# Windowed attention in a hybrid encoder layer: 192 keys for the query blocks at the grid's edges, and a moved weight copy

## The chip, the core and the metric

The kernel runs on one core of one Trainium2 chip. A core has TensorE (matmuls and transposes, results in PSUM), VectorE, ScalarE, GpSimd and SyncE, each with its own queue of instructions that it takes in order, and 16 DMA engines. The metric is device time in microseconds for one call; lower is better. In the profile TensorE is PE (its weight loads PEld), VectorE DVE, ScalarE ACT, GpSimd POOL, SyncE SP.

## The reference

One encoder layer over 512 tokens of width 2048, seen as a grid of 8 rows and 64 columns. A normalised input goes through one projection whose columns feed two groups: a gated convolution of width 31, and attention with 16 heads of 64 channels. Both are normalised, concatenated, projected and added to the residual; a gated MLP with a convolution of width 3 follows. The part that the change touches is the attention. As the grid has 8 rows and the window is 8 high, every query sees all rows, and 16 columns of them:

```python
col_start = np.clip(cols - kw // 2, 0, GRID_W - kw)        # kw = 16, GRID_W = 64
col_idx = col_start[:, None] + np.arange(kw)[None, :]
...
scores = jnp.einsum("bchd,bicjhd->bchij", q_row, k_win).astype(jnp.float32)
scores = scores + jnp.transpose(bias, (2, 0, 1, 3))[None]
p = jax.nn.softmax(scores.reshape(b, GRID_W, h, kh * kw), axis=-1)
...
return jnp.einsum("bchij,bicjhd->bchd", p, v_win)
```

A query in columns 0 to 15 sees columns 0 to 22 at most, one in columns 48 to 63 columns 40 to 63.

## The kernel before

Everything is computed in fp32 accuracy. A weight matrix is split into a rounded high part and the rest, its low part (`parts`, L129: the high part `whi` by ScalarE, L133, the low part `wlo` by VectorE, L134), the activations likewise (xh, xl), and three matmuls are added (`group`, L146: high by high L150, high by low L151, then eight low by high L153). A weight tile of 1024 columns, called a unit here, takes 24 matmuls. `weights` (L172) makes units AHEAD = 3 ahead of their use; `whi` and `wlo` have NW = 4 buffers each, the raw weights and the bias tables share NR = 9, and tiles of 2 KB a partition share NT = 75 (`t2`).

The order of the work: the projection runs unit by unit, in the order of ORDER (a letter a for a channel tile of the convolution, q for a pair of heads). After each unit, `tick` (L158) advances one step of the waiting generators, so attention work is put between units: `attend(p, ...)` for head pair p (0 to 7) and, after pair 5's projections, `group_a` (the convolution's normalisations). The convolution's 31 taps are handed to VectorE four at a time, behind each `wlo`. The tile framework then schedules each engine's instructions by priority; `pin` keeps some of them in program order, `tc.issue_after` puts the instructions of a block behind a given one, and `shifted` changes priority.

Attention for one pair of heads. The 64 columns are cut into 4 blocks of 16 columns; a query block is 16 columns by 8 rows, 128 queries. Keys and values lie in 8 groups of 8 columns (64 keys each), two groups to a chunk of 128. Each query block takes four groups, 256 keys: KEYS names for a block where they begin, in `k` itself for blocks 0 and 3, in `ks`, a copy with exchanged groups, for blocks 1 and 2. The steps:

- `turned_v` (L471): four transposes turn v; ScalarE copies it whole to vt[0] (L480) and with exchanged halves to vt[1] (L482, two copies).
- `scores` (L484): two query blocks by two heads at a time, 128 queries by 256 keys each, blocks 0 and 1 in one tile of two PSUM banks, blocks 2 and 3 in two further banks (L488).
- `softmax` (L494), for each bank (one head, two blocks, 512 wide): scaling and bias from a table on VectorE (L499), maximum (L501), two exponentials with sums on ScalarE (L504), reciprocal (L505), two scalings on ScalarE (L507).
- three ticks later (four for pairs 5 and 6), `turn` (L512): 16 transposes of 128 by 128 (L517), and `turned_p` (L521): four ScalarE copies `pt` of 512 (L525).
- one tick later, `values` (L528): 16 matmuls (L534) into one bank `po`, two chunks for each block and head, then ScalarE's copy (L572) and the split for the output projection.

The bias tables: two loads a pair on SyncE's queue (L543), each two heads by two blocks by 256 keys. Their content is laid out on the host.

Around the change: `group_a` sums the channels (L407) and adds over partitions by a matmul (L410), then squares (L222) and their sum (L261, a matmul in the bank tagged sc or tr), a root (L237), and a broadcast by matmul (L252) with a ScalarE copy (L254; the one named ra uses the bank tagged po, that of the values). L366 and L370 are the first projection at the start of the kernel. The output projection follows in `out_half`, whose matmuls have the same lines 150 to 153 and write `po`; the residual's tiles are loaded at L596. The MLP takes the time from about 600 us on (L746, L885).

Of the kernel before, what the change touches and what calls it, by code (L numbers as in the profile page):

```python
# [1 line left out]

# [1 line left out]

# [18 lines left out]
DH = 64  # L23
NA = 1024
CK = 31
WH = 8
WW = 16
# [25 lines left out]
NEG = -1.0e30  # L53
# [23 lines left out]
def layer(ctx: ExitStack, tc: tile.TileContext, xT, xn, w_0, w_in, w_out, w_up, w_down, par, tab, g3, out):  # L77
    nc = tc.nc
# [18 lines left out]

    def t4(shape, name):

        return wpool.tile(shape, F32, tag="raw", name=name, bufs=NR)  # L100
# [10 lines left out]
    def pc(name, i):  # L111
        o = POFF[name] + i
        return prm[:, o:o + 1]
# [6 lines left out]
    ps = psm.tile([P, S], F32, tag="mm", name="warm")  # L120
    for _ in range(WARM):
        nc.tensor.matmul(ps[:, :P], ones, ones, start=True, stop=True)
    ident = consts.tile([P, P], F32, name="ident")
    make_identity(nc, ident)

    def raw_unit(src, n):
        raw = t4([P, U * P], "raw")
        return raw, nc.sync.dma_start(raw[:, :n], src)

    def parts(raw, n):  # L130
        hi = wpool.tile([P, U * P], F32R, tag="whi", name="whi", bufs=NW)
        lo = wpool.tile([P, U * P], F32R, tag="wlo", name="wlo", bufs=NW)
        i = nc.scalar.activation(hi[:, :n], raw[:, :n], AF.Copy)  # L133
        j = nc.vector.tensor_sub(lo[:, :n], raw[:, :n], hi[:, :n].bitcast(F32))  # L134
# [9 lines left out]
    tight, taps = [], []  # L144

    def group(ps, ws, ms, first, last):  # L146

# [62 lines left out]
    def split(src, g, name):  # L210

        h, l = t2(name + "h", F32R), t2(name + "l", F32R)
        nc.scalar.activation(h, src, AF.Copy, scale=g)
        nc.vector.scalar_tensor_tensor(l, src, g, h.bitcast(F32), op0=ALU.mult, op1=ALU.subtract)
        return h, l

    def sum_sq(acc, src, first, to=slice(0, S)):
        if first:
            nc.scalar.activation(acc, src, AF.Square)
        else:  # L220
            q = t2("sq")[:, to]
            nc.scalar.activation(q, src, AF.Square)  # L222
            nc.vector.tensor_add(acc, acc, q)
# [42 lines left out]
    pin = tc.keep_in_program_order  # L266
# [170 lines left out]
    def grid(t, c0, w):  # L437
        return t.rearrange("p (r c) -> p r c", c=GW)[:, :, c0:c0 + w]

    def qkv(p):  # L440
# [23 lines left out]
            got.append(t)  # L464
        return got

    def attend(p, q, ks, v):


        hps = [slice(j * DH, (j + 1) * DH) for j in range(2)]  # L470
        vt, soft = [], []  # L471

        def turned_v():
            ps = psa.tile([P, NB, P], F32, tag="po", name="trv")
            for c in range(NB):
                m = nc.tensor.transpose(ps[:, c, :], v[:, c * P:(c + 1) * P], ident)
# [3 lines left out]
            nc.scalar.activation(vt[0], ps, AF.Copy)  # L480
            for hp, by in zip(hps, (slice(1, NB), slice(0, NB - 1))):
                nc.scalar.activation(vt[1][hp, :NB - 1], ps[hp, by], AF.Copy)  # L482

        def scores(b0, both, more=False):  # L484
            for i in range(2):
                b = b0 + i
                for j, hp in enumerate(hps):
                    m = nc.tensor.matmul(both[j][:, i, :], q[hp, b * P:(b + 1) * P],  # L488
                                         ks[KEYS[b][0]][hp, KEYS[b][1] * P:][:, :2 * P],
                                         start=True, stop=True)  # L490
                    if more or i or j:
                        pin(m)

        def softmax(both):  # L494
            two = tabs.pop(0)
            for j in range(2):
                tb = two[:, j]
                s = t2("s").rearrange("p (i k) -> p i k", i=2)
                nc.vector.scalar_tensor_tensor(s, both[j], DH ** -0.5, tb, op0=ALU.mult, op1=ALU.add)  # L499
# [8 lines left out]
                soft.append(s)  # L508

        pts = []  # L510

        def turn(two, more=False):  # L512
            for j in range(2):
                s, ps = soft.pop(0), two[j]
                for i in range(2):
                    for ch in range(2):
                        m = nc.tensor.transpose(ps[:, 2 * i + ch, :], s[:, i, ch * P:(ch + 1) * P], ident)  # L517
                        if more or i or j or ch:
                            pin(m)

        def turned_p(two):  # L521
            for ps in two:
                pt = t2("pt").rearrange("p (c k) -> p c k", c=4)
                with shifted(-SOONER):
                    nc.scalar.activation(pt, ps, AF.Copy)  # L525
                pts.append(pt)

        def values(po, b0, more=False):  # L528
            for i in range(2):
                b = b0 + i  # L530
                for ch in range(2):
                    for j in (1, 0):
                        hp = hps[j]
                        m = nc.tensor.matmul(grid(po, b * BLK, BLK)[hp], vt[KEYS[b][0]][:, KEYS[b][1] + ch, hp],  # L534
                                             pts[b0 + j][:, 2 * i + ch, :], start=(ch == 0), stop=(ch == 1))
                        if more or (i, ch, j) != (0, 0, 1):
                            pin(m)

        tabs = []

        def table(b0):
            tb = t4([P, 2, 2, 2 * P], "tab")
            i = nc.sync.dma_start(tb, tab[2 * p:2 * p + 2, :, b0 // 2:b0 // 2 + 2].rearrange("h p k c -> p h k c"))  # L543
            if p == 0:
                pin(i)
            tabs.append(tb)

        table(0)
        table(2)
        yield  # L550
        both = psa.tile([P, 2, 2, 2 * P], F32, tag="sc", name="sc")
        both = [both[:, j] for j in range(2)]
        more = [psa.tile([P, 2, 2 * P], F32, tag="tr", name="sc", bufs=2) for _ in range(2)]
# [8 lines left out]
        both = [both[:, j] for j in range(2)]  # L562
# [12 lines left out]
        yield  # L575

    p, n = -1, 0
# [407 lines left out]
    b = four(False)  # L985
# [6 lines left out]
    b = four(False)  # L992
# [83 lines left out]
```

## Time and profile before

| | |
|---|---|
| three timed runs | 1977.12, 1975.62, 1975.71 us; median 1975.71 |
| the profiled execution | 1976.0 us; span 1974.2 us |
| TensorE busy in the span | 1960.6 us |
| VectorE, ScalarE busy | 1611.7, 1105.8 us |
| matmuls of the scores (L488), busy | 10.4 us on k and 8.2 us on ks |
| transposes of the probabilities (L517), busy | 15.3 us |
| matmuls of the values (L534), busy | 15.7 us |

How to read it: busy is the time in which an engine worked on at least one instruction. Matmuls overlap in a pipeline, so the distance of their starts tells more than their lengths. A row of a timeline has the start in us from the span's start, the length, engine, line, operation, tiles written and read, sizes and count; in brackets stands the idle time before it and what ended that. In a group's row the count stands behind the x, then busy us and mean ns of one, then idle us before them and what ended those. The attention's pieces lie between 117 and 546 us.

### The profile page before, as it was taken

How to read it: one execution, taken by the hardware profiler on the slowest of the kernel's cores; microseconds unless marked ns; L12 is line 12 of the kernel's file. 1: busy time of each engine (PE TensorE's matmuls, PEld its weight loads, DVE VectorE, ACT ScalarE, POOL GpSimd, SP SyncE). 2: the span in 40 equal slices, each digit the busy share in tenths (PEclk: the TensorE clock that was granted, in tenths of full speed). 3: DMA queues.
4: the chain of work that ended last, by engine and by line, in shares of the span. 5: the costliest groups of instructions: out<-in, count | busy, mean ns of one | idle time of the engine just before them, and what ended most of it. 6: DMA issues, size and time to landing. Idle time of an engine off the chain costs nothing.

```text
span 1974.2 us, 27655 instructions
## 1 busy us (share of the span) xinstructions
PE 1960.6 (99%) x10141; PEld 1668.0 (84%) x10141; DVE 1611.7 (82%) x2338; ACT 1105.8 (56%) x1750; POOL 225.7 (11%) x310
## 2 busy tenths in 40 slices
PE   9999999999999999999999999999999999999998
PEld 7888888888788888888888888888888888888886
DVE  5987688787547888888989898988888898886765
ACT  6244424548525666666666666666666654554654
POOL 0111111111001111111111111111110400000000
PEclk9999999999999999999999999999999999999999
DMA  9776767766758889999999999999986977665663
GB/s 369 186 204 177 189 184 193 181 192 215 254 139 216 207 237 267 248 260 259 249 261 249 265 246 272 245 268 242 268 225 177 377 243 233 222 213 192 192 202 118
DMA packets 141817, 450.98 MB, mean 228 GB/s; under 512 B 15088, under 2 KB 23536, under 8 KB 140272
## 3 DMA queue, kind: packets, MB, share of 16 engines
q1 hardware_dynamic: 88880, 293.46, 43.8%
q0 software_dynamic: 42624, 148.92, 35.0%
q10 hardware_dynamic: 10176, 6.83, 1.1%
q8 instruction: 80, 1.31, 0.3%
q14 instruction: 57, 0.47, 0.1%
HBM read 430.27 MB, written 111.15 MB: 274 GB/s over the span
## 4 chain that ended last, share of the span: by engine, by line
PE 98%; DVE 1%; ACT 0%; DMA 0%; issue 0%; ACTq 0%; DVEq 0%
PE pu L746 43%; PE pd L885 21%; PE pj L150 7%; PE pj L151 7%; PE pj L153 7%; PE po L150 3%; PE po L151 3%; PE po L153 3%; PE po L534 1%; PE sc L488 1%; PE trp L517 1%; PE pj L366 1%; DMA we<-in_w 0%; PE trx L641 0%; PE pj L370 0%; DVE acc L407 0%
## 5 line engine op out<-in xcount | busy, mean ns | idle before, releaser
L133 ACT ACTIVATE whi<-raw 128x1024 fp32r<-128x1024 f32 x573 | 604.8, 1057 | 563.7 <-PE pj L151 166.6
L134 DVE TENSOR_TENSOR wlo<-raw,whi 128x1024 fp32r<-128x1024 f32 x573 | 699.5, 1222 | 232.5 <-ACT whi L133 192.0
L746 PE MATMUL pu<-xc,whi 128*128 128x512 f32 x2464 | 593.6, 391 | 0.0
L746 PEld LDWEIGHTS pu<-xc,whi 128*128 128x128 f32 x2464 | 451.3, 188 | 86.8 <-DVE xc L634 0.4
L746 PEld LDWEIGHTS pu<-xc,wlo 128*128 128x128 f32 x2464 | 319.2, 191 | 13.7
L746 PE MATMUL pu<-xc,wlo 128*128 128x256 f32 x2464 | 324.2, 283 | 0.0
L885 PE MATMUL pd<-whi,ho 128*128 128x512 f32 x1232 | 305.0, 389 | 0.1
L885 PEld LDWEIGHTS pd<-whi,ho 128*128 128x128 f32 x1232 | 231.1, 188 | 48.7 <-DVE vl L759 0.5
L150 PE MATMUL pj<-xh,whi 128*128 128x512 f32 x608 | 239.0, 393 | 0.0
L151 PE MATMUL pj<-xl,whi 128*128 128x512 f32 x608 | 236.9, 390 | 0.0
L392 DVE SCALAR_TENSOR_TENSOR y<-ch,prm,y 128x500 f32<-128x500 f32 (+14 forms) x240 | 177.3, 742 | 5.3
L885 PE MATMUL pd<-wlo,ho 128*128 128x512 f32 x616 | 165.1, 389 | 0.0
L153 PE MATMUL pj<-xh,wlo 128*128 128x512 f32 x608 | 150.3, 389 | 0.0
L150 PEld LDWEIGHTS pj<-xh,whi 128*128 128x128 f32 x608 | 114.1, 188 | 26.7 <-issue 2.8
L885 PEld LDWEIGHTS pd<-wlo,ho 128*128 128x128 f32 x616 | 115.6, 188 | 24.1
L153 PEld LDWEIGHTS pj<-xh,wlo 128*128 128x128 f32 x608 | 114.1, 188 | 23.7
L151 PEld LDWEIGHTS pj<-xl,whi 128*128 128x128 f32 x608 | 114.2, 188 | 23.6 <-issue 0.2
L755 ACT ACTIVATE pu<-pu 128x512 f32<-128x512 f32 x132 | 76.5, 580 | 92.9 <-PE pu L746 92.9
L695 POOL DMA_DIRECT2D raw<-in_w_up x88 | 78.0, 887 | 357.8 <-DVE wlo L134 206.7
L205 POOL DMA_DIRECT2D ws<-in_w_down x88 | 79.8, 907 | 309.1 <-DMA ws<-in_w_down 123.2
L202 POOL DMA_DIRECT2D ws<-ws x44 | 23.0, 524 | 318.1 <-PE pj L153 105.9
L202 POOL DMA_DIRECT2D ws<-in_w_down x44 | 22.9, 520 | 312.8 <-PE pj L153 172.9
(189 smaller groups left out, 1980.6 us busy)
## 6 DMA issues: line engine op xcount, KB each, us to landing
raw<-in_w_up SPq DMA_DIRECT2D x220, 512.0 KB, 5.9
ws<-in_w_down POOLq DMA_DIRECT2D x132, 512.0 KB, 6.1
raw<-in_w_up POOLq DMA_DIRECT2D x88, 512.0 KB, 7.4
raw<-ws SPq DMA_DIRECT2D x88, 512.0 KB, 4.2
raw<-in_w_in SPq DMA_DIRECT2D x76, 512.0 KB, 5.2
raw<-in_w_down SPq DMA_DIRECT2D x66, 512.0 KB, 3.8
ws<-ws POOLq DMA_DIRECT2D x44, 512.0 KB, 5.8
raw<-in_w_out SPq DMA_DIRECT2D x32, 512.0 KB, 5.3
```

The lines of the kernel that those rows point to most:

```text
L133: i = nc.scalar.activation(hi[:, :n], raw[:, :n], AF.Copy)
L134: j = nc.vector.tensor_sub(lo[:, :n], raw[:, :n], hi[:, :n].bitcast(F32))
L150: nc.tensor.matmul(ps, hi, mh, start=first and k == 0, stop=False)
L151: nc.tensor.matmul(ps, hi, ml, start=False, stop=False)
L153: i = nc.tensor.matmul(ps, lo[:, wk * P:(wk + 1) * P], mh, start=False, stop=last and k == len(ws) - 1)
L202: behind(nc.gpsimd.dma_start(wsum[c][k], a), ins)
L205: nc.gpsimd.dma_start(wsum[c][k], w_down[k, {1: A21, 2: A11, 4: A11, 6: A12}[c]], accum_op=ALU.add, max_dma_last_dim=ROW)
L392: nc.vector.scalar_tensor_tensor(y[:, a:b], h[:, a + j - PAD:b + j - PAD], prm[:, o:o + 1], y[:, a:b], op0=ALU.mult, op1=ALU.add)
L695: nc.gpsimd.dma_start(a[c], w_up[f, q2], accum_op=ALU.add)
L746: i = nc.tensor.matmul(ps[:, :n], part[:, k * P:(k + 1) * P], comb[c][k][:, :n], start=j == 0 and not more, stop=j == 2 * U - 1, skip_grou ...
L755: nc.scalar.activation(to, ps, AF.Copy)
L885: m = nc.tensor.matmul(ps[i], h[:, o + t * P:o + (t + 1) * P], w[:, d], start=start and not more and kind == 0 and j == 0, stop=stop and k ...
```

## The change

Five edits, all shown in the diff (cut):

1. The query blocks at the grid's edges, 0 and 3, take three groups of keys (192) instead of four; the middle blocks, 1 and 2, keep 256. The pairs of blocks that share a bank are now the two edge blocks (2 x 192 = 384 wide) and the two middle blocks (512).
2. The edge pair's probabilities are turned in three chunks of 128 for each head instead of four, 14 transposes a pair of heads instead of 16. The middle one of the three holds keys of both edge blocks. For it v is kept in a tile `edge` whose second and third chunks are zero in one half of the partitions; this tile is cleared once, and takes the place of vt[0]. ScalarE writes it in three copies (128x256, and twice 64x128) instead of one of 128x512. The values still take 16 matmuls.
3. The bias table holds the edge blocks (384) and one middle block (256) for each head; both middle blocks read the same one. It is loaded in two DMAs as before.
4. `turned_p` remembers its last copy in `copies`; the next weight unit's high part is issued after it on ScalarE.
5. The host lays out the table accordingly.

In the instructions as built, TensorE has 9907 instead of 9923, ScalarE 1708 instead of 1692. Ahead of the first of a pair's pt copies ScalarE has one high part fewer than before, in pair 6 three fewer; from the output projection's second half on, the order on every engine is the old one.

```diff
-KEYS = ((0, 0), (1, 0), (1, 1), (0, 2))
-WITHIN = ((0, 1, 2, 3), (1, 0, 3, 2))
+EDGE, MID = (0, 3), (1, 2)
+KEYS = ((0, 0, 3 * DH), (1, 0, 4 * DH), (1, 2 * DH, 4 * DH), (0, 5 * DH, 3 * DH))
+ATEDGE = ((0, 0), (1, 1)), ((1, 2), (2, 3))
+ATMID = ((0, 0), (1, 1)), ((2, 1), (3, 2))
...
-        i = nc.scalar.activation(hi[:, :n], raw[:, :n], AF.Copy)
+        with tc.issue_after(copies.pop().ins) if copies else nullcontext():
+            i = nc.scalar.activation(hi[:, :n], raw[:, :n], AF.Copy)
...
+    edge = t2("edge").rearrange("p (c k) -> p c k", c=NB)
+    nc.vector.memset(edge, 0.0)
...
-            vt.extend(t2("vt").rearrange("p (c k) -> p c k", c=NB) for _ in range(2))
-            nc.scalar.activation(vt[0], ps, AF.Copy)
-            for hp, by in zip(hps, (slice(1, NB), slice(0, NB - 1))):
+            vt.extend((edge, t2("vt").rearrange("p (c k) -> p c k", c=NB)))
+            nc.scalar.activation(edge[:, ::NB - 1], ps[:, ::NB - 1], AF.Copy)
+            for n, (hp, by) in enumerate(zip(hps, (slice(1, NB), slice(0, NB - 1)))):
+                nc.scalar.activation(edge[hp, n + 1], ps[hp, n + 1], AF.Copy)
                 nc.scalar.activation(vt[1][hp, :NB - 1], ps[hp, by], AF.Copy)
...
-                    m = nc.tensor.matmul(both[j][:, i, :], q[hp, b * P:(b + 1) * P],
-                                         ks[KEYS[b][0]][hp, KEYS[b][1] * P:][:, :2 * P],
+                    m = nc.tensor.matmul(both[j][:, i, :], q[hp, b * P:(b + 1) * P], ks[swapped][hp, at:at + w],
...
-                for i in range(2):
-                    for ch in range(2):
-                        m = nc.tensor.transpose(ps[:, 2 * i + ch, :], s[:, i, ch * P:(ch + 1) * P], ident)
+                for c in range(ps.shape[1]):
+                    m = nc.tensor.transpose(ps[:, c, :], s[:, c * P:(c + 1) * P], ident)
...
                 with shifted(-SOONER):
-                    nc.scalar.activation(pt, ps, AF.Copy)
+                    i = nc.scalar.activation(pt, ps, AF.Copy)
                 pts.append(pt)
+            copies[:] = [i]
...
-                        m = nc.tensor.matmul(grid(po, b * BLK, BLK)[hp], vt[KEYS[b][0]][:, KEYS[b][1] + ch, hp],
-                                             pts[b0 + j][:, 2 * i + ch, :], start=(ch == 0), stop=(ch == 1))
+                        m = nc.tensor.matmul(grid(po, b * BLK, BLK)[hp], vt[KEYS[b][0]][:, g, hp],
+                                             pt[j][:, c, :], start=n == 0, stop=n == 1)
...
-        table(0)
-        table(2)
+        we, wm = KEYS[0][2], KEYS[1][2]
+        te, tm = t4([P, 2, 2 * we], "tab"), t4([P, 2, wm], "tab")
+        for tb, at in ((te, slice(0, 2 * we)), (tm, slice(2 * we, None))):
+            i = nc.sync.dma_start(tb, tab[2 * p:2 * p + 2, :, at].rearrange("h p k -> p h k"))
...
-        scores(0, both, True)
-        scores(2, more, True)
-        softmax(both)
-        softmax(more)
+        scores(EDGE, both, True)
+        scores(MID, more, True)
+        softmax(both, we, lambda j: te[:, j].rearrange("p (i k) -> p i k", i=2))
+        softmax(more, wm, lambda j: tm[:, j].unsqueeze(1).broadcast_to([P, 2, wm]))
...
-        both = [both[:, j] for j in range(2)]
+        both = [both[:, j, :3] for j in range(2)]
...
-        values(po, 0)
-        values(po, 2, True)
+        values(po, EDGE, pts[:2], ATEDGE)
+        values(po, MID, pts[2:], ATMID, True)
```

More of the change, by code (lines that the diff above doesn't have):

```diff
@@ L1 @@
-from contextlib import ExitStack, contextmanager
+from contextlib import ExitStack, contextmanager, nullcontext
 import numpy as np
@@ L142, in unit @@
         return parts(raw_unit(src, n)[0], n)[:2]
-    tight, taps = [], []
+    tight, taps, copies = [], [], []
     def group(ps, ws, ms, first, last):
@@ L478, in turned_v, with scores @@
                     pin(m)
[L479 to L481 removed]
+            vt.extend((edge, t2("vt").rearrange("p (c k) -> p c k", c=NB)))
+            nc.scalar.activation(edge[:, ::NB - 1], ps[:, ::NB - 1], AF.Copy)
+            for n, (hp, by) in enumerate(zip(hps, (slice(1, NB), slice(0, NB - 1)))):
+                nc.scalar.activation(edge[hp, n + 1], ps[hp, n + 1], AF.Copy)
                 nc.scalar.activation(vt[1][hp, :NB - 1], ps[hp, by], AF.Copy)
[L484 to L486 removed]
+        def scores(pair, both, more=False):
+            for i, b in enumerate(pair):
+                swapped, at, w = KEYS[b]
                 for j, hp in enumerate(hps):
[L488 to L489 removed]
+                    m = nc.tensor.matmul(both[j][:, i, :], q[hp, b * P:(b + 1) * P], ks[swapped][hp, at:at + w],
                                          start=True, stop=True)
@@ L492, in scores, with softmax @@
                         pin(m)
-        def softmax(both):
-            two = tabs.pop(0)
+        def softmax(both, w, tb):
             for j in range(2):
-                tb = two[:, j]
-                s = t2("s").rearrange("p (i k) -> p i k", i=2)
-                nc.vector.scalar_tensor_tensor(s, both[j], DH ** -0.5, tb, op0=ALU.mult, op1=ALU.add)
+                flat = t2("s")[:, :2 * w]
+                s = flat.rearrange("p (i k) -> p i k", i=2)
+                nc.vector.scalar_tensor_tensor(s, both[j], DH ** -0.5, tb(j), op0=ALU.mult, op1=ALU.add)
                 nm = sm.tile([P, 2], F32, tag="nm", name="nm")
@@ L514, in turn @@
                 s, ps = soft.pop(0), two[j]
-                for i in range(2):
-                    for ch in range(2):
-                        m = nc.tensor.transpose(ps[:, 2 * i + ch, :], s[:, i, ch * P:(ch + 1) * P], ident)
-                        if more or i or j or ch:
-                            pin(m)
+                for c in range(ps.shape[1]):
+                    m = nc.tensor.transpose(ps[:, c, :], s[:, c * P:(c + 1) * P], ident)
+                    if more or c or j:
+                        pin(m)
@@ L521, in turned_p @@
         def turned_p(two):
             for ps in two:
-                pt = t2("pt").rearrange("p (c k) -> p c k", c=4)
+                pt = t2("pt")[:, :ps.shape[1] * P].rearrange("p (c k) -> p c k", k=P)
                 with shifted(-SOONER):
-                    nc.scalar.activation(pt, ps, AF.Copy)
+                    i = nc.scalar.activation(pt, ps, AF.Copy)
                 pts.append(pt)
[L528 to L531, printed above, removed]
+            copies[:] = [i]
@@ L532, in values @@
+        def values(po, pair, pt, places, more=False):
+            for i, b in enumerate(pair):
+                for n, (c, g) in enumerate(places[i]):
                     for j in (1, 0):
                         hp = hps[j]
-                        m = nc.tensor.matmul(grid(po, b * BLK, BLK)[hp], vt[KEYS[b][0]][:, KEYS[b][1] + ch, hp],
-                                             pts[b0 + j][:, 2 * i + ch, :], start=(ch == 0), stop=(ch == 1))
-                        if more or (i, ch, j) != (0, 0, 1):
+                        m = nc.tensor.matmul(grid(po, b * BLK, BLK)[hp], vt[KEYS[b][0]][:, g, hp],
+                                             pt[j][:, c, :], start=n == 0, stop=n == 1)
+                        if more or (i, n, j) != (0, 0, 1):
@@ L544, in table @@
             if p == 0:
                 pin(i)
-            tabs.append(tb)
-        table(0)
-        table(2)
         yield
-        both = psa.tile([P, 2, 2, 2 * P], F32, tag="sc", name="sc")
-        both = [both[:, j] for j in range(2)]
-        more = [psa.tile([P, 2, 2 * P], F32, tag="tr", name="sc", bufs=2) for _ in range(2)]
+        both = psa.tile([P, 2, S], F32, tag="sc", name="sc")
+        both = [both[:, j, :2 * we].rearrange("p (i k) -> p i k", i=2) for j in range(2)]
+        more = [psa.tile([P, 2, wm], F32, tag="tr", name="sc", bufs=2) for _ in range(2)]
@@ L1053 @@
     qr, qc = np.divmod(np.arange(P), BLK)
-    kg, kr, kc = np.unravel_index(np.arange(2 * P), (NB, WH, HG))
-    tab = np.full((HEADS, 3, P, 2 * P), NEG, rpb.dtype)
-    for kind, b in ((0, 0), (1, 1), (2, 3)):
+    tab = np.full((HEADS, P, 2 * KEYS[0][2] + KEYS[1][2]), NEG, rpb.dtype)
+    o = 0
+    for b in (0, 3, 1):
         c = b * BLK + qc[:, None]
-        swapped, at = KEYS[b]
-        k = ((2 * at + swapped + np.array(WITHIN[swapped])[kg]) * HG + kc)[None, :]
+        swapped, at, w = KEYS[b]
+        g = np.arange(at, at + w) // DH
+        g = g + 1 + np.where(g % 2, -1, 1) if swapped else g
+        kr, kc = np.divmod(np.arange(w) % DH, HG)
+        k = (g * HG + kc)[None, :]
         start = np.clip(c - WW // 2, 0, GW - WW)
         q_, k_ = np.nonzero((k >= start) & (k < start + WW))
-        tab[:, kind, q_, k_] = rpb[:, kr[k_] - qr[q_] + WH - 1, (k - c)[q_, k_] + WW - 1]
-    tab = np.ascontiguousarray(tab.transpose(0, 2, 1, 3))
+        tab[:, q_, o + k_] = rpb[:, kr[k_] - qr[q_] + WH - 1, (k - c)[q_, k_] + WW - 1]
+        o += w
     arrays = {"xT": xT, "xn": np.ascontiguousarray(a["x"][0]), "w_0": w_0, "w_in": w_in,
```

7 lines of the change are left out of this document (1 added, 6 removed).

## The prediction

> **What bounds the kernel now.** I read the page first: busy shares, the clock row of the slices, the chain that ended last.
>
> ```profile
> span 1974.2 us, 27655 instructions
> ...
> PE 1960.6 (99%) x10141; PEld 1668.0 (84%) x10141; DVE 1611.7 (82%) x2338; ACT 1105.8 (56%) x1750; POOL 225.7 (11%) x310
> ...
> PEclk9999999999999999999999999999999999999999
> ...
> PE 98%; DVE 1%; ACT 0%; DMA 0%; issue 0%; ACTq 0%; DVEq 0%
> ```
>
> TensorE is busy 99% of the span, at full clock in every slice, and 98% of the chain is its own work. So a microsecond of TensorE work taken out is a microsecond of the kernel, and work of the other engines counts only where TensorE waits for it. Second view: all waits of TensorE, whole kernel (engine, line, waited for: us in total, times, longest).
>
> ```profile
> PE po L534 <- ACT ra L254: 1.9, 1, 1.9
> PE pj L366 <- ACT weh L281: 1.4, 3, 0.7
> PE warm L122 <- DVE ones L117: 1.1, 1, 1.1
> PE st L410 <- DVE acc L407: 0.3, 1, 0.3
> ```
>
> Two of the four lie in the attention's stretch: one 1.9 us at the values' matmuls (L534) and one 0.3 us at the channel sum L410. Those and the attention's own matmuls are all that this change can move; nothing after about 560 us is edited, and TensorE's order there is the old one.
>
> **The change part by part.** All terms are made against the profiled execution, 1976.0 us (span 1974.2 and 1.8 around it). The median of the three timed runs, 1975.71, is 0.3 lower; I subtract that at the end.
>
> *Scores, transposes, values on TensorE.* Third view: the chain between 420 and 560 us (start, length, what), two pieces, each of one head pair. Fourth: TensorE's timeline in the same stretch (start, length, instructions).
>
> ```profile
> 470.51 1.93 PE sc L488 x16
> 495.39 1.75 PE trp L517 x16
> ```
>
> ```profile
> 423.31 1.03 PE L488 MATMUL sc<-ks,q 64*128 64x256 f32 x8
> 424.17 0.60 PE L488 MATMUL sc<-k,q 64*128 64x256 f32 x4
> ...
> 454.65 1.98 PE L153 MATMUL pj<-xh,wlo 128*128 128x512 f32 x8
> 456.55 1.97 PE L534 MATMUL po<-pt,vt 128*64 128x128 f32 x32
> ```
>
> A pair has eight score matmuls; the trace has two instructions for each, x16, and the two heads (upper and lower 64 partitions) run side by side. The eight on ks start at 423.31 and the next group at 424.17: 0.86 us for four steps, 0.215 a step of 256 keys. Four of the eight steps of a pair become 192 wide. If a step goes by its columns it takes 0.215 x 192/256 = 0.161, and a pair saves 4 x 0.054 = 0.215 us; eight pairs **1.7 us**. From below, a step can gain nothing; from above nothing beats proportion. What could hold a step at its old length is the weight load, so its rows:
>
> ```profile
> L488 PEld LDWEIGHTS sc<-ks,q 64*128 64x128 f32 x64 | 6.2, 187 | 0.7
> L517 PEld LDWEIGHTS trp<-ident,s 128*128 128x128 f32 x128 | 14.5, 141 | 1.0
> ```
>
> A load under the scores lasts 187 ns, more than 161. But a load under the transposes lasts 141 while those step at 1.75 / 16 = 0.109 us: a load's recorded length does not set the step. I take the proportional value and keep nothing as the other end. The Trainium skill (TensorE: Matmul & The Clock Gate, "LDWEIGHTS (loading the stationary operand)") speaks against the change here: a load costs by its columns, some 107 ns for 128 of them, whatever the rows. By it, were the two heads' loads of a step to run one behind the other, a step would stay near 0.214 and this term would be nothing; that is the first rival below.
>
> The edge pair's probabilities are 384 wide, so three transposes a head instead of four: two fewer a pair, 2 x 0.109 = 0.22 us, eight pairs **1.75 us**. The group's last instruction fixes no more than the hand-over, so I bound this from 1.5 to 1.75. Values keep their 16 matmuls of 128 columns (x32 at 456.55): no gain, no loss; that half of the rows in the shared block meet zeros changes no size.
>
> *The wait at 508 us.* Pair 6 (the seventh): TensorE's timeline, then ScalarE's.
>
> ```profile
> 506.51 1.98 PE L153 MATMUL po<-mah,wlo 128*128 128x512 f32 x8
> 510.40 1.97 PE L534 MATMUL po<-pt,vt 128*64 128x128 f32 x32 [1.92 <-ACT ra L254]
> ```
>
> ```profile
> 493.32 1.99 ACT L133 ACTIVATE whi<-raw 128x1024 fp32r<-128x1024 f32 x2
> 501.27 1.06 ACT L133 ACTIVATE whi<-raw 128x1024 fp32r<-128x1024 f32 x1 [5.96 <-PE po L151]
> 506.71 1.06 ACT L133 ACTIVATE whi<-raw 128x1024 fp32r<-128x1024 f32 x1 [4.38 <-PE po L151]
> 507.79 2.06 ACT L525 ACTIVATE pt<-trp 128x512 f32<-128x512 f32 x4
> 509.72 0.63 ACT L254 ACTIVATE ra<-st 128x512 f32<-128x512 f32 x1
> ```
>
> ScalarE takes its instructions in order. Ahead of the four copies of the turned blocks (pt) stand four high parts (whi); the third and fourth wait until TensorE has finished with their buffers, at 501.3 and 506.7, although the blocks were turned by 497.1 (495.39 and 1.75 in the chain). The copies and the copy of ra (which holds the bank that the values need) then run from 507.8 to 510.3, and the values start at 510.40. From the last group of eight to the values it is 3.89 us here and 1.90 elsewhere (454.65 to 456.55): the wait costs **2.0 us**. In the changed kernel as built, one high part stands ahead of pair 6's copies (the one at 493.32) and three behind the copy of ra. The copies can start when the blocks are turned, near 497, and ra is there by about 499.8, eight microseconds ahead of the values, which TensorE would then reach at 508.4. What is late next? The three held high parts: the first, ready at 494, now ends near 500.5, but its weights are those after the two units in flight and the values, needed from about 510; the other two wait for TensorE anyway. In the other seven pairs exactly one high part moves from ahead of the copies to behind them. Four high-part buffers stand against units of 5.44 us (501.27 to 506.71), so a unit has some 16 us from its buffer's release to its use; the move costs it 4 to 5. I cost it at nothing, with a bound in the third rival.
>
> *The wait at 436 us.* TensorE's and VectorE's timelines at pair 5:
>
> ```profile
> 436.14 1.10 PE L410 MATMUL st<-acc,ones 128*128 128x512 f32 x2 [0.26 <-DVE acc L407]
> ```
>
> ```profile
> 425.07 1.28 DVE L499 SCALAR_TENSOR_TENSOR s<-sc,tab 128x512 f32<-128x512 f32 x2
> ...
> 435.30 0.69 DVE L407 TENSOR_TENSOR acc<-acc,y 128x512 f32<-128x512 f32 x1
> ```
>
> VectorE is the late one: without a break from the softmax at 425.07 to the last sum at 435.9. Two bias additions (1.28 for two) and two maxima of the same width become a quarter narrower: 4 x 0.16 = 0.6 us off, less a fixed share, say 0.5. TensorE arrives 0.2 earlier, by its shorter scores. So the sum is ready first and the **0.26 us** go. Bounds 0 and 0.26.
>
> Further on in pair 5, the squares' sum (L261) now stands right behind the transposes, instead of one matmul later, and needs the bank of the edge pair's blocks, so it waits for their two copies. Those have six transposes ahead of them instead of eight and are narrower; I call it even, 0.2 either way.
>
> *What lies beside.* ScalarE: rows of the groups.
>
> ```profile
> L525 ACT ACTIVATE pt<-trp 128x512 f32<-128x512 f32 x32 | 16.5, 605 | 10.3 <-PE trp L517 10.2
> L482 ACT ACTIVATE vt<-trv 64x384 f32<-64x384 f32 x16 | 7.7, 479 | 0.1
> L480 ACT ACTIVATE vt<-trv 128x512 f32<-128x512 f32 x8 | 4.8, 595 | 8.4 <-PE trv L476 8.4
> ```
>
> From 595 at 512 wide and 479 at 384 I get 0.9 ns an element. A pair's one copy of 595 ns becomes one of 256 and two of 128 wide, estimated 0.4 + 2 x 0.28: 0.4 us more. Four exponentials and four scalings lose 64 elements each, two pt copies 128: 12 x 0.058 = 0.7 us less. ScalarE gains 0.3 us a pair, off the path. The tables: two loads a pair as before, 640 KB instead of 1 MB, in the same places of SyncE's queue. The one new VectorE instruction, the clearing of the edge tile, is put ahead of the third low part of the start; VectorE's timeline, and the chain where TensorE first reads that part:
>
> ```profile
> 23.14 1.22 DVE L134 TENSOR_TENSOR wlo<-raw,whi 128x1024 fp32r<-128x1024 f32 x1
> ```
>
> ```profile
> 28.44 1.81 PE pj L370 x8
> ```
>
> From 24.4 to 28.4 there are 4 us, which hide a clearing of 512 columns (under 0.7 us, the length of an addition of that width at L407); without that cover it would cost its length once. The edge tile holds one of 75 buffers for the whole attention, but the residual tiles' loads still follow the same last readers, so SyncE's queue isn't held longer.
>
> **Sum:** 1.7 + 1.75 + 2.0 + 0.25 = 5.7 us. 1976.0 - 5.7 = 1970.3; less 0.3 for the median: **1970.0 us**.
>
> **Rivals.**
>
> *A: the score step stays at 0.215.* For it: the load of 187 ns is longer than the new step. Against it: the transposes. It loses 1.7 us: gain 4.0, **1971.7**.
>
> *B: the wait at the values only changes its owner.* For it: pair 6's values need five copies on ScalarE, and one instruction ahead of them that waits for TensorE, as the high part at 506.71 does, holds all five. Against it: the only high part left ahead of them is that of 493.32, which waits for nothing. All of the 2.0 back: gain 3.7, **1972.0**.
>
> *C, slower: the held high part reaches VectorE.* The low part (wlo, L134) stands in VectorE's order; while it waits for the high part, the taps, the softmax and the reading of the projections' banks behind it wait too. Pair 0, ScalarE and VectorE:
>
> ```profile
> 134.95 1.06 ACT L133 ACTIVATE whi<-raw 128x1024 fp32r<-128x1024 f32 x1 [0.58 <-PE pj L151]
> 137.64 2.07 ACT L525 ACTIVATE pt<-trp 128x512 f32<-128x512 f32 x4 [1.62 <-PE trp L517]
> ```
>
> ```profile
> 138.52 1.22 DVE L134 TENSOR_TENSOR wlo<-raw,whi 128x1024 fp32r<-128x1024 f32 x1
> ```
>
> The copies, 0.4 earlier and 0.2 shorter by the terms above, end near 139.1; the high part moves from 134.95 to behind them and ends near 140.1, so this wlo starts 1.6 us later. Two taps have been put ahead of it and fill most of that; VectorE loses under a microsecond a pair and has gained 0.5. It would be slower only if each pair passed over 1.2 us to TensorE (9.7 over eight pairs: the 5.7 gained and 4 more); were the whole move of 4.2 us (134.95 to 139.1) exposed eight times, it would be 34 - 5.7 = 28 us, **1998**. VectorE's idle time between 110 and 420 us speaks against it:
>
> ```profile
> 110.00:420.00 310.00, 310.00 (x1566) 255.85 (x1565) 245.85 (x341) 130.47 (x242) 35.84 (x51) 1.00 0.71 188
> ```
>
> TensorE is busy 310.00 of 310 us there, VectorE 245.85: 64 us idle for five pairs, 13 each.
>
> *D: nothing to be measured:* scores, transposes and the wait all come back elsewhere, **1975.7**. Against it: no cover of TensorE exists in which they could vanish.
>
> **How the numbers follow.** Forecast 0.66, A 0.12, B 0.12, C 0.04, D 0.03, and 0.03 for a gain beyond the terms. The forecast's own spread: terms from 5.2 to 6.2, so 1969.5 to 1970.5. The range reaches over A and B with that spread: **1969.2 to 1972.5**, which leaves out C, D and a little of both ends. A measurement of this kernel tells about 0.2%, 3.95 us, from no change: the line is 1971.8. The forecast lies under it whole, A about half, the extra gain whole: faster 0.66 + 0.07 + 0.03 = 0.76. Same: the rest of A, B and D, 0.05 + 0.12 + 0.03 = 0.20. Slower: C, 0.04.
>
> **What the changed profile would show.** Score groups of a pair at 1.7 us instead of 1.93, with the eight edge instructions 0.16 us a step (A if they keep 0.215). Fourteen transposes in 1.53. TensorE's waits without L534 (B if a row of 1 us or more is left there) and without L410. ScalarE's pt copies of pair 6 near 497, well ahead of the values. C would show as new TensorE waits on wlo or on VectorE's readings between 110 and 560 us. The prediction is wrong if the span between the first score and the last value shrinks by less than 4 us, or if what shrinks there comes back after 560.

## The result and the profile after

The changed kernel takes 1970.02 us (median of 7 runs, 1969.65 to 1970.17), the kernel before beside it 1976.08 (7 runs, 1975.62 to 1977.61): a ratio of 0.9967, 95% interval [0.9958, 0.9977]. The forecast was 1970.0 in 1969.2 to 1972.5. The profiled execution took 1970.17 us, 5.8 less than that of before.

The page of the changed kernel: span, busy shares, and the engines' shares of the chain that ended last.

```profile
span 1968.4 us, 27634 instructions
...
PE 1956.4 (99%) x10125; PEld 1665.2 (85%) x10125; DVE 1608.1 (82%) x2339; ACT 1100.9 (56%) x1766; POOL 225.3 (11%) x310
...
PE 98%; DVE 1%; DMA 0%; issue 0%; ACT 0%; ACTq 0%; DVEq 0%
```

TensorE's busy time fell by 4.2 us (1960.6 to 1956.4) with 16 instructions fewer; the span fell by 5.8. By these numbers 4.2 us of the gain are less work and 1.6 us are waiting that is gone; measured from start to start, further down, the split is 3.4 and 2.4. Still TensorE carries the chain. All of its waits, whole kernel (waited for: us in total, times, longest):

```profile
PE pj L369 <- ACT weh L284: 1.8, 2, 1.3
PE warm L124 <- DVE ones L119: 1.1, 1, 1.1
PE st L264 <- DVE acc L226: 0.2, 1, 0.2
```

The rows of the values and of the channel sum are gone; one of 0.2 us at the squares' sum is new. (1.9 and 0.3 less, 0.2 more here and 0.4 more in the first row: the 1.6.) The first row lies at the kernel's start and differs from one execution to the next (1.1 to 2.0 us over the profiles of this study), whatever the kernel. To keep that out, I compare kernels by one distance inside the trace: from the first pair's turned values to the first transpose of x after the output projection. TensorE's timeline has both starts:

```profile
117.73 0.60 PE L482 MATMUL trv<-ident,v 128*128 128x128 f32 x4
...
596.26 0.60 PE L640 MATMUL trx<-ident,x 128*128 128x128 f32 x4
```

That is 478.53 us. Before, the same two groups:

```profile
117.61 0.60 PE L476 MATMUL trv<-ident,v 128*128 128x128 f32 x4
...
602.02 0.60 PE L641 MATMUL trx<-ident,x 128*128 128x128 f32 x4
```

That is 484.41: the attention's stretch is 5.88 us shorter, and what follows it has its old length (1372.2 and 1372.1 us). So this distance holds the whole gain.

The pieces. The chain, for one pair of heads each (start, length, what):

```profile
467.62 1.71 PE sc L495 x16
...
492.28 1.53 PE trp L521 x14
...
505.15 1.90 PE po L538 x32
```

Scores 1.93 to 1.71, transposes 1.75 to 1.53, values 1.90 as before. From start to start of the groups in the trace it is 1.927 to 1.714 in all eight pairs, and 1.665 to 1.447 in seven of them. The instructions of the scores, by form (ns min/median/max of one):

```profile
L495 PEld LDWEIGHTS sc<-k,q x64: 182/186/187, 118.3 to 513.5; 64*128 64x128 f32 x64
L495 PE MATMUL sc<-k,q x64: 322/323/427, 118.3 to 513.7; 64*128 64x192 f32 x64
...
L495 PE MATMUL sc<-ks,q x64: 376/376/376, 119.0 to 514.5; 64*128 64x256 f32 x64
```

A 192-wide instruction is 53 ns shorter than a 256-wide one, with a weight load as long as ever (186). Four steps of a pair shortened by 53 ns make 0.213 us.

Pair 6, TensorE, ScalarE:

```profile
503.18 1.98 PE L156 MATMUL po<-mah,wlo 128*128 128x512 f32 x8
505.08 1.09 PE L538 MATMUL po<-pt,edge 128*64 128x128 f32 x16
```

```profile
489.79 1.05 ACT L136 ACTIVATE whi<-raw 128x1024 fp32r<-128x1024 f32 x1
492.97 1.85 ACT L529 ACTIVATE pt<-trp 128x384 f32<-128x384 f32 x4 [2.13 <-PE trp L521]
494.68 0.63 ACT L257 ACTIVATE ra<-st 128x512 f32<-128x512 f32 x1
495.16 1.10 ACT L136 ACTIVATE whi<-raw 128x1024 fp32r<-128x1024 f32 x1
497.94 1.06 ACT L136 ACTIVATE whi<-raw 128x1024 fp32r<-128x1024 f32 x1 [1.69 <-PE po L154]
503.38 1.06 ACT L136 ACTIVATE whi<-raw 128x1024 fp32r<-128x1024 f32 x1 [4.38 <-DMA x<-in_xT]
```

The values now start 1.90 behind the last group of eight, as in the other pairs. The copies run as soon as the blocks are turned and are done by 494.8, ra by 495.3, ten microseconds ahead of the values. The three high parts that stood ahead of them follow, two of them still waiting for their buffers, but with nothing urgent behind them (the last row names a DMA; it stands a unit of 5.44 us behind the one before it, as it did before the change).

Pair 5, TensorE at the channel sum and at the squares' sum:

```profile
431.58 1.98 PE L156 MATMUL pj<-xh,wlo 128*128 128x512 f32 x8
433.39 1.07 PE L413 MATMUL st<-acc,ones 128*128 128x512 f32 x2
...
445.24 1.69 PE L521 MATMUL trp<-ident,s 128*128 128x128 f32 x14
447.13 1.02 PE L264 MATMUL st<-ones,acc 128*128 128x1 f32 x8 [0.20 <-DVE acc L226]
```

The last group of eight ahead of the channel sum, before:

```profile
433.90 1.97 PE L153 MATMUL pj<-xh,wlo 128*128 128x512 f32 x8
```

The channel sum started 2.24 us behind it (433.90 to 436.14); now 1.81, which is eight steps of 0.227 and no wait. So that wait was worth 0.42 (2.236 less 1.814), though its row said 0.26: a row of waits counts idle time from the modelled end of the last matmul (435.88), and the next one could have started before that end, as it does now (1.81 behind a group whose modelled length is 1.98). At the squares' sum 0.2 appear. From the transposes to the values pair 5 takes 8.42 instead of 8.56: a gain of 0.14 where the other pairs have 0.22.

The sum: scores 8 x 0.213 = 1.71, transposes 7 x 0.218 + 0.14 = 1.66, the values' wait 1.99, the channel sum's 0.42: 5.78 of 5.88; the other 0.1 is spread, and no piece of it is over 0.04.

### The profile page after: what moved, and what is told of

It is laid out like the page before. It is cut to its first block, busy times and chain, and to the rows that moved or that the text cites. A ratio compares the mean times of both kernels' runs of the same rounds, so it can differ in the third digit from the quotient of the medians.

```text
span 1968.4 us, 27634 instructions
## 1 busy us (share of the span) xinstructions
PE 1956.4 (99%) x10125; PEld 1665.2 (85%) x10125; DVE 1608.1 (82%) x2339; ACT 1100.9 (56%) x1766; POOL 225.3 (11%) x310
## 4 chain that ended last, share of the span: by engine, by line
PE 98%; DVE 1%; DMA 0%; issue 0%; ACT 0%; ACTq 0%; DVEq 0%
PE pu L745 44%; PE pd L884 21%; PE pj L153 7%; PE pj L154 7%; PE pj L156 7%; PE po L153 3%; PE po L154 3%; PE po L156 3%; PE po L538 1%; PE sc L495 1%; PE pj L369 1%; PE trp L521 1%; DMA we<-in_w 0%; PE trx L640 0%; PE pj L373 0%
```

## The experiments

Eight kernels ran; "distance" is the one defined above. Each ratio is to runs of the kernel before that were made beside it.

| kernel | median us (runs) | ratio to before | distance us |
|---|---|---|---|
| the changed kernel | 1970.02 (7) | 0.9967 [0.9958, 0.9977] | 478.53 |
| e1_no_hold | 1971.49 (9) | 0.9975 [0.9966, 0.9985] | 480.33 |
| e2_hold_only | 1973.66 (11) | 0.9986 [0.9977, 0.9995] | 482.41 |
| e4_16_turns | 1971.54 (10) | 0.9976 [0.9967, 0.9986] | 480.30 |
| e3_128_keys | 1963.73 (5) | 0.9938 [0.9924, 0.9951] | 472.28 |
| e6_two_maxima | 1970.49 (6) | 0.9969 [0.9958, 0.9981] | 479.25 |
| e5_hold_ao | 1970.94 (7) | 0.9974 [0.9963, 0.9984] | 479.69 |
| e7_hold_ao_but_4 | 1970.27 (5) | 0.9966 [0.9953, 0.9978] | 478.52 |
| e8_hold_ao_4 | 1970.56 (7) | 0.9969 [0.9958, 0.9981] | 479.27 |

Differences of medians and of distances part by some tenths, e1's for instance 1.47 and 1.80: the first pair's turned values start at 117.1 to 117.8 us in the ten profiles, and the distance leaves that out.

The theory is the prediction's: four terms, each of its own cause. Its rivals: the score step is held by the weight load; the wait at the values only changes its owner; the held high part reaches TensorE by way of VectorE.

**e1_no_hold and e2_hold_only: the order on ScalarE, taken away and put alone.** e1 is the changed kernel with edit 4 undone:

```diff
-        with tc.issue_after(copies.pop().ins) if copies else nullcontext():
-            i = nc.scalar.activation(hi[:, :n], raw[:, :n], AF.Copy)
+        i = nc.scalar.activation(hi[:, :n], raw[:, :n], AF.Copy)
```

> The changed kernel without the order edge: the next high part is again free to stand ahead of the turned blocks' copies (as built, 86 high parts ahead of pair 6's copies instead of 83). My theory, that the 2.0 us wait at pair 6's values came from high parts that wait for TensorE ahead of the copies: the wait is back, 1970.0 + 2.0 = 1972.0 us, scores and transposes stay short. Rival, that the narrower blocks relieved ScalarE enough to end the wait: 1970.0 us and no wait at the values.

e2 is the kernel before with edit 4 alone (these lines the other way, and `copies[:] = [i]` behind the pt copies).

> The kernel before with the order edge alone, 256 keys everywhere. My theory: the wait at pair 6's values goes, 1976.1 - 2.0 = 1974.1 us; scores keep 1.93 and transposes 1.75 us a pair; the wait at L410 (0.3 us) stays, since VectorE's work is the old one. Rival, that the narrower blocks ended the wait: 1976.1 us. If it is the order alone that ended L410's wait as well, that row is gone here too and the time is 1973.7.

e1, TensorE's waits (without the two of the start), then ScalarE's and TensorE's timeline at pair 6; the three high parts stand ahead of the pt copies again, the last of them from 503.00 on:

```profile
PE po L537 <- ACT ra L256: 1.7, 1, 1.7
...
PE st L263 <- DVE acc L225: 0.2, 1, 0.2
```

```profile
504.09 1.85 ACT L528 ACTIVATE pt<-trp 128x384 f32<-128x384 f32 x4
505.80 0.63 ACT L256 ACTIVATE ra<-st 128x512 f32<-128x512 f32 x1
```

```profile
506.48 1.09 PE L537 MATMUL po<-pt,edge 128*64 128x128 f32 x16 [1.70 <-ACT ra L256]
```

The wait is back at the same place with the same owner, and it is the only group that differs from the changed kernel by more than 0.04: 1.77 us. In the kernel before it was 1.99; the four pt copies are 0.21 shorter now (2.06 to 1.85), as two of them are 384 wide. So narrower blocks alone would have given 0.2 of the 2.0. In e2 the same stretch is 1.99 shorter and the distance 2.00. Its waits:

```profile
PE st L411 <- DVE acc L408: 0.3, 1, 0.3
```

Beside the two rows of the start that is the only one. The values' row is gone and nothing took its place, so rival B is out. The channel sum's wait stays (2.23 behind the eight): the order on ScalarE does nothing for it. In e1, with the narrower blocks and without the order, that wait is gone (1.81).

**e4_16_turns: the transposes by themselves.** The changed kernel with four transposes for each head of the edge pair, the fourth over columns already turned and read by nobody:

```diff
-                for c in range(ps.shape[1]):
-                    m = nc.tensor.transpose(ps[:, c, :], s[:, c * P:(c + 1) * P], ident)
+                for c in range(4):
+                    o = min(c * P, s.shape[-1] - P)
+                    m = nc.tensor.transpose(ps[:, c, :], s[:, o:o + P], ident)
...
```

> The changed kernel with the edge pair turned in four chunks a head (the fourth repeats columns of the third and is not read), 16 transposes a pair instead of 14; all other engines have the same work. My theory, that each transpose is worth its 0.109 us on TensorE: 1970.0 + 16 x 0.109 = 1971.8 us. Rival, that another engine sets the pace of this stretch and TensorE's saving was not what moved the time: 1970.0 us.

The distance is 1.77 longer, and in the chain a pair's transposes have their old length:

```profile
136.39 1.75 PE trp L522 x16
```

So each transpose left out is worth 0.109 us, all of it on the path.

**e3_128_keys: does the gain go on by columns?** The edge blocks take 128 keys; the third group of keys is left out of the computation.

```diff
-KEYS = ((0, 0, 3 * DH), (1, 0, 4 * DH), (1, 2 * DH, 4 * DH), (0, 5 * DH, 3 * DH))
-ATEDGE = ((0, 0), (1, 1)), ((1, 2), (2, 3))
+KEYS = ((0, 0, 2 * DH), (1, 0, 4 * DH), (1, 2 * DH, 4 * DH), (0, 6 * DH, 2 * DH))
+ATEDGE = ((0, 0),), ((1, 3),)
...
```

> One size changed: the edge blocks take 128 keys instead of 192 (the third group of keys is left out of the computation), so a pair has 12 transposes and 12 matmuls of the values. My theory, that all goes by columns: four score steps of 0.108 instead of 0.161 (0.21 us a pair), two transposes (0.22) and four matmuls of the values, four steps of 0.109 (0.44): 0.87 a pair, 8 pairs 6.9 us, 1963.1 us. Rival, that the weight load (187 ns) keeps a score step from going under some 0.16: 1.7 us less of it, 1964.8 us, with score steps still at 0.16.

The scores by form, then the pieces of a pair in the chain:

```profile
L495 PEld LDWEIGHTS sc<-k,q x64: 182/187/188, 117.8 to 507.6; 64*128 64x128 f32 x64
L495 PE MATMUL sc<-k,q x64: 272/272/373, 117.8 to 507.7; 64*128 64x128 f32 x64
```

```profile
117.90 1.51 PE sc L495 x16
135.96 1.31 PE trp L521 x12
142.74 1.46 PE po L538 x24
```

The score group falls again by 0.20, from 1.714 to 1.511 start to start, while the load still lasts 187 ns: rival A is out, with room to spare. Four steps of 64 columns less are worth 0.213 the first time and 0.203 the second, 0.8 ns a column. By the Trainium skill (TensorE: Matmul & The Clock Gate, "LDWEIGHTS (loading the stationary operand)") a load of 128 columns costs some 107 ns; an estimate from that figure is that a step could not fall under 0.214 if the loads of the two heads ran one behind the other. Here they don't: by the groups the step fell by 53 and then 51 ns from 0.216, to 0.112, and in the first pair's trace the two heads' loads of a step start 6 or 7 ns apart. Nor does a recorded load last 107 ns; it lasts 182 to 188.

Scores, transposes and values add up to 8 x (0.203 + 0.219 + 0.437) = 6.87 us, and the distance fell by 6.25. What is missing stands in TensorE's timeline and VectorE's at pair 5:

```profile
426.74 1.98 PE L156 MATMUL pj<-xh,wlo 128*128 128x512 f32 x8
429.27 1.10 PE L413 MATMUL st<-acc,ones 128*128 128x512 f32 x2 [0.56 <-DVE acc L410]
```

```profile
426.57 1.23 DVE L137 TENSOR_TENSOR wlo<-raw,whi 128x1024 fp32r<-128x1024 f32 x1
427.71 1.41 DVE L410 TENSOR_TENSOR acc<-acc,y 128x512 f32<-128x512 f32 x2
```

The sum waits 0.72 (2.53 behind the eight instead of 1.81), of which 0.3 come back between pair 5's transposes and its values (7.91 us instead of 8.42, where 0.22 were due); the other 0.2 are lost in pieces of some 0.02 a pair. The cause of the wait: in this kernel a low part of 1.2 us stands ahead of the last two channel sums, where in the changed kernel all the sums come first. Less work on TensorE turned into a wait for VectorE, as soon as VectorE's order at that place was worse by one instruction.

**e6_two_maxima: is it VectorE's width that ends the channel sum's wait?** The maximum of the edge blocks is taken twice.

```diff
-                nc.vector.tensor_reduce(nm, s, axis=AX.X, op=ALU.max, negate=True)
+                for _ in range(2 if w < 2 * P else 1):
+                    nc.vector.tensor_reduce(nm, s, axis=AX.X, op=ALU.max, negate=True)
```

> The changed kernel with the edge pair's maximum taken twice on VectorE, about 0.54 us more for each of 16, 1.1 us a pair: more than the narrower softmax gave VectorE. My theory, that VectorE counts only where TensorE waits for the channel sums in pair 5: those two places lose up to 1.1 us together, 1970.2 to 1971.2 us, and nothing elsewhere. Rival, that VectorE's relief is what moved the time: 16 x 0.54 = 8.6 us more, 1978.6 us.

VectorE and TensorE at pair 5:

```profile
422.78 1.92 DVE L507 TENSOR_REDUCE nm<-s 128x2 f32<-128x384 f32 x4
```

```profile
433.96 1.10 PE L413 MATMUL st<-acc,ones 128*128 128x512 f32 x2 [0.74 <-DVE acc L410]
```

VectorE is 0.92 longer there (1.92 against 1.00 for two), and the stretch from the scores to the channel sum grew by 0.90. So in the changed kernel VectorE is on time by no more than 0.02 us. The traces say the same directly: in e3, e5, e6 and e8, and in the kernel before, the channel sum starts 0.145 to 0.147 behind the end of VectorE's last addition; in the changed kernel it starts 0.169 behind it. In the seven other pairs the same 0.92 costs nothing at all; some 0.2 come back at pair 5's squares' sum, so that the distance is 0.72 longer. VectorE added to all pairs counts in one.

**e5_hold_ao, e7_hold_ao_but_4, e8_hold_ao_4: the slower rival.** If the held high part can reach TensorE by way of VectorE, a longer hold should show it. e5 holds it behind ao, the copy of the values, in all pairs; the next high part then starts some 7 us later against the turned blocks' copies, in pair 6 13 us:

```diff
-            copies[:] = [i]
+            held[:] = [1]
...
-        nc.scalar.activation(ao, po, AF.Copy)
+        i = nc.scalar.activation(ao, po, AF.Copy)
+        held.clear()
+        copies[:] = [i]
```

(and no further unit is made while `held` is set).

> The changed kernel with the next unit's high part held back further, behind the copy of the pair's result (ao) instead of the turned blocks' copies, some 8 us later in each pair. My theory, that a unit's high part has about 16 us from its buffer's release to its use: no change, 1969.7 to 1970.4 us, no new wait of TensorE on low parts. Rival, that the hold is near its price already: TensorE waits at the low parts, 1 us or more a pair, 1978 us or more.

The distance is 1.16 longer: 0.67 at pair 5's channel sum and 0.44 at pair 6. Neither expectation fits: not the theory's nothing, and far from the rival's 8 us. VectorE at pair 4 and at pair 5 in e5:

```profile
388.87 1.23 DVE L137 TENSOR_TENSOR wlo<-raw,whi 128x1024 fp32r<-128x1024 f32 x1 [4.59 <-ACT whi L136]
...
420.92 1.22 DVE L137 TENSOR_TENSOR wlo<-raw,whi 128x1024 fp32r<-128x1024 f32 x1
```

In the changed kernel the two low parts up to the same place stand so:

```profile
414.94 1.23 DVE L137 TENSOR_TENSOR wlo<-raw,whi 128x1024 fp32r<-128x1024 f32 x1 [0.67 <-PE pj L156]
...
420.39 1.23 DVE L137 TENSOR_TENSOR wlo<-raw,whi 128x1024 fp32r<-128x1024 f32 x1 [1.24 <-PE pj L156]
```

In e5 VectorE starves for 4.6 us behind the late high part, works without a break from then on, and reaches the low part at 420.92 late by 0.7 against pair 5's turned values (0.96 behind them instead of 0.26). Thirty microseconds lie between the starving and the loss. That asks two things: is it pair 4's hold, and do the other pairs' holds cost nothing? e7 holds behind ao in pairs 0 to 3 and 7 only, e8 in pair 4 only:

```diff
-            copies[:] = [i]
+            held[:] = [1] if p not in (4, 5, 6) else []
+            copies[:] = [] if held else [i]
...
-            copies[:] = [i]
+            held[:] = [1] if p == 4 else []
+            copies[:] = [] if held else [i]
```

> The changed kernel, with the next unit's high part held behind the copy of the values (ao) instead of behind the turned blocks' copies in the five pairs 0, 1, 2, 3 and 7; pairs 4, 5 and 6 keep the hold of the changed kernel. Held behind ao in all eight pairs, the kernel lost 0.9 us (1970.94 against 1970.02). Theory: only a hold that ends within about 30 us of the channel sums (L413) counts, as the VectorE time it costs is otherwise made up in VectorE's idle time before anything of TensorE needs it. So 1970.0, no wait at L413, the distance from the first to the last pair's turned values within 0.2 of 478.53. Rival: every pair hands some 0.1 us of its hold to TensorE; then five of eight pairs give 0.6, 1970.6, in small waits between 110 and 560 us.

> The changed kernel, with the next unit's high part held behind the copy of the values (ao) in pair 4 alone. Theory: VectorE starves behind the held high part at 388 us, has no idle time from there to the channel sums of pair 5, and is late there by 0.7 us: a wait of about 0.5 us at L413 and 1970.7. Rival: the wait at L413 comes from pair 5's own hold, which is made in the same stretch; then no wait at L413 and 1970.0.

e7 has the changed kernel's distance to 0.01 (478.52) and no row at the channel sum. Its median, 1970.27, lies 0.25 higher, within the scatter of its runs (1969.69 to 1970.97). e8 is 0.73 longer, 0.68 of it at the channel sum. VectorE in e8 at the hold, then TensorE at the sum:

```profile
388.47 1.23 DVE L137 TENSOR_TENSOR wlo<-raw,whi 128x1024 fp32r<-128x1024 f32 x1 [4.59 <-ACT whi L136]
```

```profile
431.00 1.97 PE L156 MATMUL pj<-xh,wlo 128*128 128x512 f32 x8
433.50 1.10 PE L413 MATMUL st<-acc,ones 128*128 128x512 f32 x2 [0.52 <-DVE acc L410]
```

2.50 from the eight to the sum instead of 1.81. So the mechanism of the slower rival exists, and it costs where TensorE asks VectorE for a sum before VectorE's idle time has made up for the hold; elsewhere that idle time takes it up. The stretches of e7 and of the changed kernel show that (for each stretch: us, busy time of PE, PEld, DVE, ACT, POOL with counts, clock, DMA share, GB/s):

```profile
321.00:360.00 39.00, 39.00 (x214) 32.21 (x213) 27.10 (x41) 19.91 (x45) 3.48 (x6) 1.00 0.67 171
360.00:420.00 60.00, 60.00 (x305) 49.57 (x304) 52.44 (x74) 24.91 (x50) 7.50 (x11) 1.00 0.70 192
```

```profile
321.00:360.00 39.00, 39.00 (x215) 32.20 (x213) 31.79 (x48) 20.12 (x45) 4.36 (x7) 1.00 0.67 178
360.00:420.00 60.00, 60.00 (x305) 49.56 (x304) 47.88 (x67) 24.91 (x50) 6.56 (x10) 1.00 0.70 187
```

VectorE does 4.7 us less in the first stretch (pair 3's hold) and 4.6 more in the second, and TensorE is busy throughout in both. No run takes the 0.44 at pair 6 of e5 apart. Its trace points to pair 5's hold: VectorE starves again, for 4.44 us up to the low part at 457.77, and pair 6's first exponential on ScalarE starts 15.39 us behind its scores instead of 13.49 (483.45 and 468.06; in the changed kernel 481.04 and 467.55), before pair 6's own hold begins behind its copies at 493.5.

## Why the prediction was right

**Scores, 1.7 us predicted, 1.71 measured.** The step went by its columns, as taken; e3 carried it on to 128. The argument used against rival A, that a load's recorded length does not set the step, holds: the load lasts 186 ns under steps of every width.

**Transposes, 1.75 predicted, 1.66 measured.** 0.218 in seven pairs, 0.14 in pair 5, where the squares' sum stands right behind them and waits 0.2 for VectorE. The text called that place even, 0.2 either way; it cost 0.08. The prediction had the squares' sum wait for two ScalarE copies; the second of these ends at 446.97 and VectorE's last square at 446.99, and the row names VectorE. So the place and the size held, but the engine that comes last is VectorE, if only by 0.02 us. e4 gives the whole term back.

**The wait at the values, 2.0 predicted, 1.99 measured.** e2 shows that the order alone does it, e1 that without the order it stays. The shorter copies alone would have taken 0.2 of it (e1).

**The channel sum, 0.25 predicted, 0.42 measured.** The mechanism was right: e2 leaves the wait where it was, e1 is rid of it without the order, and e6 brings it back by VectorE's work alone. Its size was off, and the upper bound of 0.26 with it, since I read it from the row of waits; for the values' wait I had measured from start to start. VectorE got 0.66 us shorter from the low part at the turned values to the last sum (before, that low part starts at 422.50 and the next one behind the sums at 435.91, 13.41; now 12.75), TensorE arrives 0.21 earlier: the difference, 0.45, is the 0.42 of the wait and a margin of 0.02, within rounding. Of the 0.66, 0.54 are the narrower additions and maxima, 1.28 and 1.27 for two before, and in VectorE's timeline now

```profile
422.19 1.01 DVE L504 SCALAR_TENSOR_TENSOR s<-sc,tab 128x384 f32<-128x384 f32 x2
423.12 1.00 DVE L506 TENSOR_REDUCE nm<-s 128x2 f32<-128x384 f32 x2
```

(0.5 in the prediction); the rest is in small gaps.

**What lies beside.** ScalarE's busy time fell by 4.9 us (predicted 0.3 a pair, 2.4). It had room, and nothing on the path shows it. Nor does the clearing of the edge tile show: the first pair's turned values start at 117.1 to 117.8 us in the eight profiles that have it, at 117.3 and 117.6 in the two that don't.

**The slower rival, C.** With the hold as it is made, no wait for a low part shows in any pair. The prediction argued from VectorE's 64 idle microseconds over five pairs. That was right for the sum over pairs, but it is not what decides: between pair 4's hold and pair 5's channel sum the longer hold uses up all of VectorE's idle time, and 0.7 us of it are left over. The dearest case given for C, 1998, is also added wrongly: 28 us on top of the 1975.7 of before are 2004, the 5.7 having been taken off twice.

**The total, 5.7 predicted, 5.8 to 5.9 measured.** Transposes 0.1 under, channel sum 0.17 over, 0.1 spread. That the median, 1970.02, meets the forecast to 0.02 is partly luck: the terms came out 0.1 to 0.2 larger, and the 0.3 taken off for the median was 0.15 (1970.17 profiled, 1970.02 the median), and the two errors cancel.

## What to carry to other kernels

Where one engine carries the chain, price an edit by the distance from start to start of that engine's groups, not by a row of idle time, which counts from a modelled end and showed 0.26 of 0.42 us here. In a queue taken in order, an instruction that waits for a buffer belongs behind the one whose result is wanted first: that ordering alone gave 2.0 us, more than either cut of work in this change (1.71 and 1.66). A delay on an engine with idle time costs nothing until the one place where the bound engine waits for it, so look for that place, and for the idle time between the delay and it, instead of the idle time in all.

## What was not expected

A delay on VectorE was carried for 30 us, from 388.5 to 420.5, without a trace on TensorE in between, and came out 13 us later as 0.68 us at the channel sum (e8). And the margin that the changed kernel has at this sum is 0.02 us: four of the eight experiments, which touch three different things (fewer keys in e3, a second maximum in e6, a later high part in e5 and e8), each lost 0.67 to 0.90 us at this one matmul.
